# A hybrid attention decoder layer: three of sixteen gate projections computed beside the other attention

## Chip, cores and metric

The kernel runs on one core of a Trainium2 chip. The metric is the device time of one execution in microseconds. TensorE is called PE here (its weight loads PEld), VectorE DVE, ScalarE ACT, GpSimd POOL and SyncE SP, as in the profile.

## What is computed

One decoder layer on 1024 tokens of 1024 channels, all in float32. One input projection gives the queries, keys and values of two attention branches and two gates; branch A is a causal attention with a forget bias, branch B a sparse attention that keeps 256 keys per query; both are gated, summed, projected, and a SwiGLU follows.

```python
proj = x @ w_in[l]
(fq, fk, fv, f_logit, dq, dk, dv, iq, ik, iw, g_a, g_b) = _split_columns(proj)
o_a = _fox_attention(fq, fk, fv, f_logit + b_forget[l])     # 8 heads of 64
o_b = _dsa_attention(dq, dk, dv, iq, ik, iw)                # 8 heads of 64, top-k of indexer scores
...
merged = (jax.nn.sigmoid(g_a) * (o_a @ w_branch_a[l])
          + jax.nn.sigmoid(g_b) * (o_b @ w_branch_b[l]))
x = _layer_norm(ALPHA * x + merged @ w_out[l], ln1_g[l], ln1_b[l])
```

## The kernel before

Every float32 matmul is made of three: each operand is split into a high and a low part, and high x high, low x high and high x low are summed in PSUM (`mm3`, L99 to L101). A weight chunk of 128 columns is loaded by SP (L88), its high part made by ACT and its low part by POOL (`load_w`, L92 and L93).

After the input projections of the indexer come the two attentions, up to 800 us. They are done as 64 items in the order of the list `todo`: unit n (0 to 7) is a pair of heads, units 0 to 3 of the forgetting branch (items 0 to 31) and units 4 to 7 of the sparse branch (items 32 to 63); within a unit each of two heads goes through four pairs G of query blocks in the order 3, 0, 2, 1, so that four items in a row always make the same work, and the large ones are G = 3 and G = 2. An item has two parts. `weigh` makes the scores of its two query blocks (S, L456 to L459) and the softmax: for the forgetting branch a maximum on DVE (L466), an exponential on ACT (L467); for the sparse branch DVE adds the selection mask and takes the maximum (L469) and ACT makes the exponential (L472); then a reciprocal on DVE (L473) and the division on POOL (p, L476). `average` transposes p on PE (T, L499), splits the result on ACT (ph, L500) and DVE (pl, L501) and multiplies it with V (O, L508 and L509). The scores of the next item are made in the middle of the averaging of the present one, in slots; how many are before the transposes of the next item is fixed by `A1`.

Beside that PE does filler work: the projection of the next unit's queries, keys and values (48 steps) and the gate projections (16 steps each; 16 gates). A step is one `mm3` over 128 input channels for 512 tokens, three matmuls. A gate ends with two tanh evictions on ACT (L377) and two stores (L378). A projection of queries, keys and values ends with evictions on ACT and DVE (L392 and L393, L403 and L404, L428 and L429). `NG` says how many gates are done beside each unit; the steps of a unit are spread evenly over its eight items:

```python
total = [16 * g + (48 if n < 7 else 0) for n, g in enumerate(NG)]
...
    goal = sum(total[:n]) + total[n] * part // (2 * sum(W)) + lead * (64 - k) // 64
    for x, g in enumerate(slots):
        next(g, None)
        fill(work, at0 + (goal - at0) * (x + 1) // len(slots))
```

Beside each unit the gates come first, then the projection of the next unit.

PE's order is this order, word for word (`manual_schedule`). The other engines are ordered by a scheduler at build time that fills an engine whenever it finds it free. What it fills with in the forgetting half is the top-k selection, which needs only the indexer's scores: for query blocks 2, 3 and 4 by 32 rounds of max and replace on DVE (L287, L288), for blocks 5, 6 and 7 by a bisection of 32 rounds, in which ACT counts (L307) and DVE makes the next threshold (L308, L317, L315); at its end DVE turns the scores into a mask (L319 to L358). The sparse half begins only after that.

Of the kernel before, what the change touches and what calls it, by code (L numbers as in the profile page):

```python
# [36 lines left out]

NMM, NT = 2, 2
AHEAD, LASTC = 4, 6
NG = (1, 1, 2, 2, 2, 2, 2, 4)  # L40
ORDER = (3, 0, 2, 1)
PHB, PLB = 3, 3
A1 = (1, 2, 2, 2)
# [6 lines left out]
def trunk_kernel(ctx: ExitStack, tc: tile.TileContext, xT, xn, wt, wbr, wout, wfi, wfo,  # L50
# [506 lines left out]
    def filler():  # L557

        count = 0
        for n in range(8):  # L560
            for g in [gates.pop(0) for _ in range(NG[n])] + \
                    ([project(*divmod(n + 1, 4), units[n + 1])] if n < 7 else []):
# [8 lines left out]

    total = [16 * g + (48 if n < 7 else 0) for n, g in enumerate(NG)]
    done = [0]
# [395 lines left out]
```

## Time and profile before

| | us |
|---|---|
| median of 3 runs (1711.6 to 1712.47) | 1711.94 |
| the profiled execution | 1713.46 |
| its span, first to last instruction | 1711.70 |
| PE busy | 1632.9 |
| DVE busy | 1067.9 |
| ACT busy | 770.1 |
| POOL busy | 639.2 |

Busy time is the time in which an engine runs an instruction. Matmuls overlap in PE's pipeline, so how long one takes is read from the start of one to the start of the next. An engine works through its instructions in order; the time that it stood idle ahead of one is shown in brackets with what ended the wait.

### The profile page before, as it was taken

Reading aid. Unit: us, or ns where it says so; the run is one execution under the profiler, and the core shown is the slowest. Engines: PE = TensorE matmul, PEld = TensorE weight load, DVE = VectorE, ACT = ScalarE, POOL = GpSimd, SP = SyncE. Lnnn points to the kernel's source line nnn. Section 1 sums busy time; section 2 is a strip of 40 time slices with the busy share of each in tenths; the row PEclk is TensorE's granted clock in tenths of the full one; section 3 lists DMA queues with packets and bytes.
Section 4 is the critical chain, followed back from the end, with each engine's and each line's share of the span. In section 5 each row is a group of like instructions: output and inputs, shape, how many; then the busy total and the mean of one; then the engine's idle time right before and its main releaser. Section 6 shows DMA issues by size and latency. Waiting matters only on the chain.

```text
span 1711.7 us, 22054 instructions
## 1 busy us (share of the span) xinstructions
PE 1632.9 (95%) x7806; PEld 1335.1 (78%) x7806; DVE 1067.9 (62%) x1875; ACT 770.1 (45%) x1375; POOL 639.2 (37%) x617
## 2 busy tenths in 40 slices
PE   7898999998999999999989988999999998899998
PEld 5776887776888888887867866888888887788886
DVE  6889999969545454545376588744444443545655
ACT  6777878783545454455231033233333331433430
POOL 1123333332333333333340048644444442553751
PEclk9999999999999999999999998999999999899999
DMA  5112212221212121215875113322222220753641
GB/s 180 40 44 61 58 50 53 69 57 48 75 50 75 58 70 57 68 57 192 282 235 195 50 50 101 110 85 87 81 80 79 82 74 36 265 192 122 228 141 62
DMA packets 66326, 171.06 MB, mean 100 GB/s; under 512 B 7908, under 2 KB 12004, under 8 KB 66216
## 3 DMA queue, kind: packets, MB, share of 16 engines
q1 hardware_dynamic: 66216, 169.66, 30.6%
q8 instruction: 61, 1.00, 0.2%
q14 instruction: 49, 0.40, 0.1%
HBM read 123.67 MB, written 37.04 MB: 94 GB/s over the span
## 4 chain that ended last, share of the span: by engine, by line
PE 72%; DVE 13%; ACT 5%; DMA 4%; issue 3%; POOL 1%; SPq 0%; DVEq 0%; ACTq 0%; POOLq 0%
PE pb L100 8%; PE pb L101 8%; PE pb L99 8%; PE mm L99 6%; PE mm L100 6%; PE mm L101 6%; PE acc L100 5%; PE acc L99 5%; PE acc L101 5%; PE T L499 3%; PE ob L100 2%; PE ob L101 2%; PE ob L99 2%; DVE sm L288 2%; PE O L509 2%
## 5 line engine op out<-in xcount | busy, mean ns | idle before, releaser
L99 PE MATMUL mm<-xh,whi 128*128 128x512 f32 (+1 forms) x720 | 296.6, 412 | 15.6 <-ACT whi L144 6.2
L101 PE MATMUL mm<-xl,whi 128*128 128x512 f32 (+1 forms) x720 | 281.7, 392 | 0.8 <-DVE xl L154 0.7
L100 PE MATMUL mm<-xh,wlo 128*128 128x512 f32 (+1 forms) x720 | 281.2, 391 | 0.5 <-DVE wlo L145 0.5
L476 POOL TENSOR_SCALAR p<-p,st 128x512 f32<-128x512 f32 (+1 forms) x192 | 113.3, 599 | 321.3 <-DVE st L473 265.9
L93 POOL TENSOR_TENSOR wlo<-wraw,whi 128x1024 fp32r<-128x1024 f32 x51 | 123.1, 2414 | 192.7 <-ACT whi L92 192.5
L101 PEld LDWEIGHTS mm<-xl,whi 128*128 128x128 f32 x720 | 136.1, 189 | 31.8 <-DVE xl L154 2.0
L99 PEld LDWEIGHTS mm<-xh,whi 128*128 128x128 f32 x720 | 137.1, 190 | 30.1 <-issue 6.4
L776 POOL TENSOR_TENSOR w<-ss,w 128x512 fp32r<-128x512 f32 x88 | 118.8, 1357 | 106.4 <-ACT w L775 81.6
L99 PE MATMUL acc<-foh,hh 128*128 128x512 f32 x352 | 138.3, 393 | 10.8 <-ACT hh L883 10.8
L100 PEld LDWEIGHTS mm<-xh,wlo 128*128 128x128 f32 x720 | 137.4, 191 | 12.9 <-DVE wlo L145 1.0
L93 POOL TENSOR_TENSOR fol<-wraw,foh 128x1024 fp32r<-128x1024 f32 x44 | 108.2, 2464 | 101.3 <-ACT foh L92 70.3
L884 DVE TENSOR_TENSOR hl<-hr,hh 128x512 fp32r<-128x512 f32 x44 | 93.0, 2126 | 84.8 <-ACT hh L883 84.8
L100 PE MATMUL acc<-foh,hl 128*128 128x512 f32 x352 | 138.1, 392 | 0.0
L101 PE MATMUL acc<-fol,hh 128*128 128x512 f32 x352 | 137.9, 392 | 0.0
L501 DVE TENSOR_TENSOR pl<-T,ph 128x512 fp32r<-128x512 f32 (+1 forms) x160 | 100.6, 634 | 36.5 <-ACT ph L500 34.6
L776 POOL TENSOR_TENSOR w<-wraw,w 128x512 fp32r<-128x512 f32 x44 | 59.0, 1346 | 157.6 <-PE ob L101 86.2
L500 ACT ACTIVATE ph<-T 128x512 fp32r<-128x512 f32 (+1 forms) x160 | 87.2, 552 | 38.9 <-PE T L499 34.6
L307 ACT ACTIVATE junk<-sm,nt 128x1024 bf16<-128x1024 f32 (+2 forms) x93 | 96.8, 1041 | 14.6 <-DVE nt L315 12.8
L775 ACT ACTIVATE w<-ss 128x512 fp32r<-128x512 f32 x88 | 54.8, 629 | 102.4 <-PE pb L101 92.1
L499 PE MATMUL T<-identf,p 128*128 128x128 f32 x576 | 90.6, 273 | 4.8 <-POOL p L476 2.5
L499 PEld LDWEIGHTS T<-identf,p 128*128 128x128 f32 x576 | 71.2, 140 | 26.8 <-POOL p L476 4.5
L92 ACT ACTIVATE foh<-wraw 128x1024 fp32r<-128x1024 f32 x44 | 46.4, 1059 | 99.1 <-DMA wraw<-in_wfo_dram 56.9
(256 smaller groups left out, 3997.8 us busy)
## 6 DMA issues: line engine op xcount, KB each, us to landing
wraw<-in_wt_dram SPq DMA_DIRECT2D x45, 512.0 KB
wraw<-in_wfo_dram SPq DMA_DIRECT2D x44, 512.0 KB
wraw<-in_wfi_dram SPq DMA_DIRECT2D x26, 512.0 KB
wup<-in_wfi_dram SPq DMA_DIRECT2D x22, 512.0 KB
hdr<-h SPq DMA_DIRECT2D x22, 512.0 KB
hr<-hdr SPq DMA_DIRECT2D x44, 256.0 KB
gdr<-g SPq DMA_DIRECT2D x32, 256.0 KB
g<-gdr SPq DMA_DIRECT2D x32, 256.0 KB
```

The lines of the kernel that those rows point to most:

```text
L93: pool.tensor_tensor(lo, raw, f(hi), op=OP.subtract)
L99: te.matmul(ps, ah, bh, start=(first and i == 0), stop=False)
L100: te.matmul(ps, al, bh, start=False, stop=False)
L101: te.matmul(ps, ah, bl, start=False, stop=(last and i == n - 1))
L307: act.activation(j[:, :128 * (i + 1)], SM[i], AF.Sign, bias=bias(x), accum_out=s[:, x:x + 1])
L476: pool.tensor_scalar(pc, pc, st[:, 3:4], 1.0, op0=OP.mult, op1=OP.mult)
L499: te.transpose(T[:, s * 128:s * 128 + 128], P[qq][:, j * 128:j * 128 + 128], identf)
L500: act.activation(ph[:, c:], T[:, c:], AF.Copy)
L501: dve.tensor_tensor(pl[:, c:], T[:, c:], f(ph[:, c:]), op=OP.subtract)
L775: act.activation(s[:, 0], raw, AF.Copy)
L776: pool.tensor_tensor(s[:, 1], raw, f(s[:, 0]), op=OP.subtract)
L884: dve.tensor_tensor(hl, hr, f(hh), op=OP.subtract)
```

## The change

`NG`, the number of gates beside each unit, is changed. Beside the forgetting branch (units 0 to 3) there are nine gates instead of six, beside the sparse branch seven instead of ten.

```diff
-NG = (1, 1, 2, 2, 2, 2, 2, 4)
+NG = (1, 2, 3, 3, 1, 1, 2, 3)
```

What each group of items has beside it, counted in the built order (steps between the first score matmul of the first item and that of the item after the last; the other counts are DVE's instructions):

| items | before | after |
|---|---|---|
| 8 to 15 | 62 steps; 52 max and replace, 24 of the bisection, 12 projection evictions | 76 steps; 64, 28, 11 |
| 16 to 19 | 38 steps | 46 steps |
| 20 to 23 | 39 steps | 47 steps |
| 24 to 27 | 39 steps; the 59 instructions of the selection's end, 30 of attention, 4 projection evictions | 47 steps |
| 22 to 25 (second cycle's middle) | | 48 steps; the 59 instructions of the selection's end, 30 of attention, 9 projection evictions |
| 28 to 31 | 40 steps | 48 steps |
| 36 to 39 | 40 steps | 32 steps |
| 60 to 62 | 27 steps | 20 steps |

PE, forgetting half: the first place in which the two orders differ, in unit 1, after the last score of a block (S) and ahead of the transposes of p.

```order
 L458 MATMUL S<-cmask,identb 128x128
 L459 MATMUL S<-K_1378,Q_1377 128x256
+L99 MATMUL mm<-xh_79,whi 128x512
+L100 MATMUL mm<-xh_79,wlo 128x512
+L101 MATMUL mm<-xl_81,whi 128x512
 L499 MATMUL T<-identf,p 128x128 x4
```

One step more stands between the scores and the transposes.

PE, sparse half: what stands behind the second score of item 58 (unit 7), up to the first multiplication with V, before:

```order
L459 MATMUL S<-K_7158,Q_7157 128x384
L99 MATMUL mm<-xh_79,whi 128x512
L100 MATMUL mm<-xh_79,wlo 128x512
L101 MATMUL mm<-xl_81,whi 128x512
L99 MATMUL mm<-xh_79,whi 128x512
L100 MATMUL mm<-xh_79,wlo 128x512
L101 MATMUL mm<-xl_81,whi 128x512
L508 MATMUL O<-ph,V 128x256
```

and after:

```order
L459 MATMUL S<-K_7220,Q_7219 128x384
L99 MATMUL mm<-xh_79,whi 128x512
L100 MATMUL mm<-xh_79,wlo 128x512
L101 MATMUL mm<-xl_81,whi 128x512
L508 MATMUL O<-ph,V 128x256
```

Two steps have become one; the rest up to the transposes of item 58 is the same.

DVE, forgetting half: the first scan of the selection's end (L353, L354) with what stands among it, before:

```order
L353 SCALAR_TENSOR_TENSOR cum<-e 128x512
L501 TENSOR_TENSOR pl<-T,ph 128x512
L466 TENSOR_REDUCE st<-S 128x1
L354 SCALAR_TENSOR_TENSOR e<-cum,s_4393,e 128x512
L501 TENSOR_TENSOR pl<-T,ph 128x512
```

and after:

```order
L501 TENSOR_TENSOR pl<-T,ph 128x512
L404 TENSOR_TENSOR K_3271<-mm,K_3269 64x512
L354 SCALAR_TENSOR_TENSOR e<-cum,s_4573,e 128x512
L346 TENSOR_SCALAR s_4573<-s_4573 128x1
L501 TENSOR_TENSOR pl<-T,ph 128x512
L404 TENSOR_TENSOR K_3275<-mm,K_3273 64x512
L466 TENSOR_REDUCE st<-S 128x1
```

The evictions of a projection of keys (K, L404) now stand among the selection's end.

## Rows read from the trace of the kernel before

**Rows 1.** The page's slices: busy tenths of 40 equal slices of the span.

```profile
PE   7898999998999999999989988999999998899998
DVE  6889999969545454545376588744444443545655
```

**Rows 2.** Stretches: length, busy PE, PEld, DVE, ACT, POOL (count), clock, DMA share, GB/s.

```profile
216.00:292.80 76.80, 73.91 (x411) 59.56 (x410) 75.39 (x176) 62.17 (x129) 26.37 (x46) 1.00 0.20 57
292.80:336.00 43.20, 41.68 (x228) 33.74 (x227) 41.94 (x95) 35.81 (x72) 14.78 (x21) 1.00 0.16 56
336.00:378.70 42.70, 41.56 (x226) 33.96 (x225) 30.97 (x73) 36.87 (x76) 13.41 (x24) 1.00 0.27 69
378.70:431.40 52.70, 45.38 (x235) 35.67 (x234) 48.84 (x104) 23.25 (x49) 16.19 (x22) 0.97 0.14 46
431.40:473.20 41.80, 41.80 (x229) 34.57 (x228) 22.56 (x40) 20.40 (x41) 14.46 (x25) 1.00 0.27 71
```

**Rows 3.** PE's timeline: start us, us, instruction; two steps in a row.

```profile
419.52 0.40 PE L99 MATMUL mm<-xh,whi 128*128 128x512 f32 x1
...
420.21 0.39 PE L99 MATMUL mm<-xh,whi 128*128 128x512 f32 x1
```

**Rows 4.** PE's timeline: two of its waits, idle time and releaser in brackets.

```profile
385.87 0.47 PE L99 MATMUL mm<-xh,whi 128*128 128x512 f32 x1 [2.02 <-DVE V L429]
...
414.47 0.44 PE L456 MATMUL S<-K,Q 128*128 128x384 f32 x1 [2.05 <-ACT p L467]
```

**Rows 5.** DVE's timeline: first and last instruction of the selection's end.

```profile
386.15 0.16 DVE L319 TENSOR_SCALAR u<-u 128x3 int32<-128x3 int32 x1
...
430.42 2.64 DVE L358 TENSOR_SCALAR sm<-sm 128x256 f32<-128x256 f32 x1
```

**Rows 6.** Groups by line, 216 to 433 us: count, busy us, mean ns, idle before.

```profile
L287 DVE MAX8 m<-sm 128x8 f32<-128x640 f32 (+1 forms) x47 | 36.5, 776 | 0.2
...
L404 DVE TENSOR_TENSOR K<-mm,K 64x512 fp32r<-64x512 f32 x8 | 5.5, 686 | 2.4 <-ACT K L403 2.2
L429 DVE TENSOR_TENSOR V<-mm,V 128x256 fp32r<-128x256 f32 x10 | 4.1, 413 | 0.4 <-ACT V L428 0.3
...
L92 ACT ACTIVATE whi<-wraw 128x1024 fp32r<-128x1024 f32 x12 | 12.7, 1057 | 0.0
```

**Rows 7.** Timelines of DVE and POOL around 316 us.

```profile
316.46 1.81 DVE L315 SCALAR_TENSOR_TENSOR nt<-u,mp 128x3 int32<-128x3 int32 x1
...
315.86 2.39 POOL L93 TENSOR_TENSOR wlo<-wraw,whi 128x1024 fp32r<-128x1024 f32 x1 [3.65 <-ACT whi L92]
```

**Rows 8.** Timeline: first step after an item's second score, division, transposes (items 36, 58, 60).

```profile
520.53 0.40 PE L99 MATMUL mm<-xh,whi 128*128 128x512 f32 x1
...
524.83 1.36 POOL L476 TENSOR_SCALAR p<-p,st 128x512 f32<-128x512 f32 x2 [4.92 <-DVE st L473]
...
526.02 0.60 PE L499 MATMUL T<-identf,p 128*128 128x128 f32 x4
...
745.16 0.40 PE L99 MATMUL mm<-xh,whi 128*128 128x512 f32 x1
...
748.03 1.14 POOL L476 TENSOR_SCALAR p<-p,st 128x512 f32<-128x512 f32 x2 [3.00 <-DVE st L473]
...
748.75 0.60 PE L499 MATMUL T<-identf,p 128*128 128x128 f32 x4
...
762.02 0.40 PE L99 MATMUL mm<-xh,whi 128*128 128x512 f32 x1
...
765.37 1.36 POOL L476 TENSOR_SCALAR p<-p,st 128x512 f32<-128x512 f32 x2 [3.27 <-DVE st L473]
...
766.12 0.60 PE L499 MATMUL T<-identf,p 128*128 128x128 f32 x4
```

**Rows 9.** PE's timeline: a wait in the last item, at the multiplication with V.

```profile
798.41 0.38 PE L509 MATMUL O<-pl,V 128*128 128x256 f32 x1 [0.45 <-DVE pl L501]
```

## Prediction

> **What bounds the kernel now.** I read the page first. TensorE (PE) is the engine with the fewest gaps: a slice is 42.8 us, and its digits fall below 9 in slices 1, 2, 4 and 10 and then not before slice 18. VectorE's (DVE) digits are 8 and 9, with one 6, in slices 2 to 10 and only 3 to 5 in slices 11 to 20 [rows 1]. The two places that the change touches are the forgetting half (items 0 to 31, to 473 us) and the sparse half (items 32 to 63, to 800 us). To see what each costs I cut the trace at the first score matmul of every fourth item, because four items always make the same attention work, and read the busy times of each stretch [rows 2].
>
> In items 28 to 31 PE is busy for all of 41.8 us: nothing is waited for. That gives the price of four items with 40 steps of projection beside them, 41.8 us. One step (three matmuls) lasts 0.69 to 0.70 us from start to start [rows 3]. So PE's own time for four items with n steps is 41.8 - 0.70 x (40 - n), and what a stretch takes beyond that is waiting. With the steps counted in the order: items 8 to 15 have 62 steps, own time 71.0, taken 76.8, so 5.8 us of waiting; items 16 to 19 have 38, 40.4 of 43.2, 2.8; items 20 to 23 have 39, 41.1 of 42.7, 1.6; items 24 to 27 have 39, 41.1 of 52.7, 11.6 us. Together 21.8 us of waiting before the change [rows 2].
>
> Who is waited for: in items 8 to 15 DVE is busy for 75.39 of 76.8 us, and in items 24 to 27 for 48.84 of 52.7. DVE carries the top-k selection there beside the softmax, and PE waits for DVE's results (2.02 us for the eviction of V) or for a softmax that stood behind DVE (2.05 us) [rows 4]. The last part of the selection, L319 to L358, stands from 386.15 to 433.06 us [rows 5]; it is 40 us before the sparse half begins, so its end itself holds up nothing. In items 20 to 23 DVE has 12 us to spare; there ScalarE's counting passes set the pace (36.87 of 42.7 us busy), with little waiting.
>
> **What is moved.** 48 steps of 0.70 us, 33.5 us of PE time, leave the sparse half and go to the forgetting half. PE has to do them in either place, so this by itself is worth nothing: PE's total stays. The gates bring no DVE work, but each brings a weight load, its two splits (ScalarE and GpSimd, POOL), two tanh evictions and two stores. ScalarE has at least 5.8 us to spare in each stretch, POOL is busy for a third of each and DMA for at most 27% [rows 2], so I cost these at nothing. If that cover were gone, three splits at 1.06 us and six tanh evictions at no more than that would be 9.5 us of ScalarE [rows 6]. On SP's queue a store waits for its tanh, and the weight loads behind it wait with it; these are asked for while the chunk before is still being multiplied, 16 steps or 11 us ahead. What counts is how the waiting changes.
>
> Items 8 to 15. The order puts 76 steps there in place of 62: own time 80.8 us. But it also puts more selection there: 64 instead of 52 max and replace instructions and 28 instead of 24 of the bisection, less one eviction. A max takes 0.78 us [rows 6], and I take the replace that follows each alike; one of the bisection's small ones takes 0.16 [rows 5]; an eviction 0.69. This is 12 x 0.78 + 4 x 0.16 - 0.7 = 9.3 us, and DVE comes to 75.4 + 9.3 = 84.7, still more than PE's own time. With the 1.4 us that the stretch took beyond DVE's busy time, 86.1 us, and 5.3 us of waiting instead of 5.8. Bounds: 1.6 (as in items 20 to 23, if DVE just stops binding) and 6.4.
>
> Items 16 to 21. The counting passes set the pace, as before in items 20 to 23 with 1.6 us per four items: 2.4 us for six items. Before, eight items had 4.4. Bounds 1.0 and 4.4.
>
> The selection's end. Its 59 instructions stand beside the scores of items 22 to 25 now, instead of items 24 to 27. PE has 48 steps there, own time 47.4 us. DVE has the same 59, the same 30 of attention, and nine instead of four evictions of projections, since the projection of the next pair of heads falls into the same place: four more of K at 0.69 us and one of V at 0.41, 3.2 us [rows 6]. If the stretch takes 52.7 + 3.2 = 55.9 us, the wait is 8.5 us, 3.1 less than before. But the load is uneven: counted up to the first score of item 25, DVE's instructions add up to 9 us more than PE's; with the 3.9 us by which this stretch exceeded DVE's busy time before, that is 13. I take 10.5, between them; ends 8.5 and 14.8 (nothing of the longer PE work helps, 11.6 + 3.2).
>
> Items 26 to 31 wait for nothing, as items 28 to 31 do now. Sum for the forgetting half: 5.3 + 2.4 + 10.5 = 18.2 us of waiting instead of 21.8: 3.6 us gained (between 10.7 gained and 3.8 lost).
>
> One thing speaks against the move. At 316.46 a DVE instruction on three numbers per partition took 1.81 us; a weight split on POOL had begun 0.60 us before it, and both ended at about 318.25 [rows 7]. About one more split (one per 16 steps) now falls before the selection's end: 0 to 1.7 us of DVE time, and I take 0, since the busy times above hold such hits already. The Trainium skill (SBUF — State Buffer, Who interferes with whom) says that a DVE instruction with two SBUF inputs and a GpSimd instruction that reads SBUF exclude each other for the whole instruction; the trace agrees. By that rule alone every added split could cost its full length once, and the forecast would be about 2 us later.
>
> The sparse half. There PE never waits, but by little. Between an item's second score and its transposes the chain runs over DVE, ScalarE, DVE and POOL, and PE must have that much other work. At item 58 PE's work lasts 748.75 - 745.16 = 3.59 us and the chain to the end of POOL's first of two instructions 748.60 - 745.16 = 3.44; at item 60, 4.10 and 4.03; at item 36, 5.49 against 4.98 [rows 8]. The change takes one step out of this gap at items 58 and 60 and two at items 62, 36, 40 and 44. So items 58 and 60 wait 0.6 us each, and item 62, which is like item 58 with one step more in the gap and loses two, 0.6 as well. Items 36, 40 and 44 come to 4.1 us against chains of 4.0 to 5.0: 0 to 0.9 each, I take 0.2, since most chains are at the low end. The last pair waits 0.45 us already [rows 9]; with a step less, 0.6 more. Together 3.0 us lost, bounds 1.5 and 7.
>
> **The sum.** 3.6 gained and 3.0 lost: 0.6 us faster. The profiled execution took 1713.46 us, 1.76 of it around the span of 1711.70, and would come to 1712.9. It lies 1.5 us above the median of 1711.94, and against the median I say 1711.3 us.
>
> **The rivals.** Faster: the denser filler gives DVE so much more time per item that it no longer binds in items 8 to 21, and the selection's end takes the lower end. Then 1.6 + 1.5 + 8.5 = 11.6 us of waiting are left, 10.2 gained, less 3.0: 1711.9 - 7.2 = 1704.7 us. For it: from item 8 to the end of the selection PE's own work is 193.6 us beside 197.1 of DVE busy [rows 2]; with the change the selection ends two items earlier but with 15 steps more done, 10.5 us of PE less the attention of two items, while DVE's load shrinks by the softmax of two items. Summed over the whole, PE would be the longer. Against it: the order lets the selection run ahead whenever PE is slower, so DVE stays full where it was full.
>
> Slower: the thin gap in the sparse half. If chains like item 36's (4.98) are the rule once items follow each other faster, because evictions and tanh come between, the twelve large items of units 4, 5 and 7 wait 0.5 us more each, and 9 us are lost instead of 3.0: 1711.9 - 3.6 + 9.0 = 1717.3 us. It decides from the point where the chain is longer than PE's work in the gap, 4.1 us in units 4 and 5 and 2.9 to 3.4 in unit 7. For it: item 36, 0.5 us from waiting with two steps more. Against it: items 58 and 60 ran at the shorter chains at eight steps per item.
>
> Nothing: the waits move along with the selection, their sum stays near 21.8, and the sparse half loses nothing that can be measured: 1711.9 us. This lies in the same band as the forecast.
>
> **Chances.** A measurement of this kernel tells about 0.2%, 3.4 us, from no change. Forecast 0.34, nothing 0.11, together 0.45 for the same; faster 0.31; slower 0.24. The bounds of the terms add up to -9.2 and +10.8 us, which is not likely on one side at once; 1704.5 to 1718.0 holds the rivals' times and leaves out about two in ten.
>
> **What would show it.** In the trace of the changed kernel: the sparse half, from the first score of item 32 to that of item 60, shorter by the moved work; items 8 to 15 at about 86 us with DVE full; the stretch with L319 to L358 as the one with most waiting, some 10 us; PE waits of about 0.6 us for POOL's p at the transposes of items 58, 60 and 62. I am wrong if the stretch with the selection's end shows under 6 us of waiting or over 14, or if the large items of units 4 and 5 wait too.

## The result, and the profile after

The changed kernel takes 1721.59 us (median of 4 runs, 1720.76 to 1722.84) against 1712.20 for the kernel before beside it: ratio 1.0053, 95% interval 1.0036 to 1.0071. It is slower by 9 us, and outside the range of the prediction. The profiled execution took 1722.84 us, 1721.1 of it span, 9.4 more than the span before.

The page's slices for PE and DVE hardly differ from [rows 1]:

```profile
PE   7899999998999999999998988999999999899998
DVE  6889999969345454555375689744444443455655
```

So the trace was cut again at the first score matmuls, with the columns of [rows 2]. These are items 8 to 15, 16 to 19, 20 to 23, 24 to 27 and 28 to 31 of the changed kernel:

```profile
216.00:301.10 85.10, 82.48 (x453) 67.41 (x452) 83.39 (x194) 67.26 (x138) 28.85 (x47) 1.00 0.21 63
301.10:349.10 48.00, 47.30 (x253) 38.37 (x252) 43.75 (x100) 38.97 (x80) 15.60 (x22) 1.00 0.20 66
349.10:402.40 53.30, 48.30 (x251) 38.20 (x250) 39.86 (x92) 35.75 (x72) 16.09 (x23) 1.00 0.22 61
402.40:455.60 53.20, 48.68 (x259) 39.05 (x258) 32.99 (x62) 20.24 (x43) 17.18 (x23) 1.00 0.16 55
455.60:503.00 47.40, 47.40 (x254) 39.09 (x253) 20.66 (x38) 21.91 (x44) 15.45 (x23) 1.00 0.26 74
```

Items 28 to 31 again wait for nothing. The selection's end stands where it was forecast, in items 22 to 25; the first and last instruction on DVE's timeline, to be held against [rows 5]:

```profile
378.37 0.17 DVE L319 TENSOR_SCALAR u<-u 128x3 int32<-128x3 int32 x1
...
426.51 0.28 DVE L358 TENSOR_SCALAR sm<-sm 128x256 f32<-128x256 f32 x1
```

The new thing is in the sparse half. PE's waits there (us in total, times, longest), 503 to 808 us:

```profile
PE T L499 <- POOL p L476: 6.1, 7, 1.3
PE ob L99 <- ACT g L377: 2.3, 1, 2.3
```

Before, the same list, from 473 to 801.5 us so that it too takes in the branch stage's first matmul (`ob`):

```profile
PE ob L99 <- ACT g L377: 0.7, 1, 0.7
PE O L509 <- DVE pl L501: 0.5, 1, 0.5
```

**A ledger.** Moved steps lengthen one stretch and shorten another by 0.70 us each. What a stretch's length changed beyond that is a loss (+) or a gain (-). Here it is against the kernel before, for the changed kernel and all that was run, from one profiled execution each. The stretches begin at the first score of item 0, of item 32 and of item 56, at the branch stage's first matmul, and at the first matmul behind that stage and the output projection, which is counted with it. For the changed kernel the first entry, for example, is 29.7 us longer for 46 steps more: 29.7 - 32.2 = -2.5.

| kernel | items 0-31 | items 32-55 | item 56 to branch stage | branch stage | rest | ratio of times |
|---|---|---|---|---|---|---|
| changed kernel | -2.5 | +5.7 | +3.5 | +2.0 | +0.6 | 1.0053 |
| e1_low_on_dve | -2.7 | +3.7 | +3.6 | -0.6 | -0.2 | 1.0025 |
| e2_early6 | -2.6 | +0.7 | +3.4 | +1.8 | +1.0 | 1.0013 |
| e3_late2 | -2.6 | +0.5 | +3.6 | +1.4 | 0.0 | 1.0008 |
| e4_unit4_only | -6.6 | +2.0 | +0.2 | -0.7 | +0.2 | 0.9969 |
| e5_unit4_late2 | -5.9 | +0.1 | +0.6 | -1.4 | +0.6 | 0.9958 |
| e6_unit7_only | -6.5 | 0.0 | +3.6 | +0.9 | +0.6 | 0.9983 |
| e7_unit2 | -4.7 | +1.7 | +0.2 | +1.3 | +0.3 | 0.9980 |
| e8_unit3 | +1.1 | +1.7 | +0.8 | -0.3 | +1.0 | 1.0006 |
| e9_two_u12 | -2.4 | +0.5 | +0.3 | +0.8 | +0.7 | 0.9994 |
| e10_two_u1 | -5.0 | +0.5 | -0.2 | +1.1 | +0.5 | 0.9975 |
| e11_two_u01 | -7.0 | +0.6 | 0.0 | -0.7 | +0.4 | 0.9961 |
| e12_cast_dve | -2.5 | +5.7 | +1.9 | +3.6 | +0.7 | 1.0039 |

The row of the changed kernel adds up to 9.3 of the 9.4 us. The runs' ratios have intervals of about 0.001 to each side; a ledger's sum, which rests on one execution of each kernel, lies up to 3.3 us from what its ratio says. Beside the experiments the kernel before took 1714.6 to 1715.1 us, some 2.5 us more than beside the changed kernel, which did not run again; so times are compared as ratios.

### The profile page after: what moved, and what is told of

Read it like the earlier page. It is cut to its first block, busy times and chain, and to the rows that moved or that the text cites. A ratio compares the mean times of both kernels' runs of the same rounds, so it can differ in the third digit from the quotient of the medians.

```text
span 1721.1 us, 22044 instructions
## 1 busy us (share of the span) xinstructions
PE 1633.4 (95%) x7806; PEld 1334.7 (78%) x7806; DVE 1068.8 (62%) x1875; ACT 769.9 (45%) x1375; POOL 641.4 (37%) x617
## 4 chain that ended last, share of the span: by engine, by line
PE 71%; DVE 15%; ACT 6%; issue 3%; DMA 3%; POOL 2%; SPq 0%; DVEq 0%; ACTq 0%; POOLq 0%
PE pb L100 8%; PE pb L101 8%; PE pb L99 8%; PE mm L99 6%; PE mm L101 6%; PE mm L100 6%; PE acc L99 5%; PE acc L100 5%; PE acc L101 5%; PE T L499 3%; PE ob L100 2%; PE ob L101 2%; PE ob L99 2%; DVE sm L288 2%; DVE m L287 2%
## 5 line engine op out<-in xcount | busy, mean ns | idle before, releaser
L476 POOL TENSOR_SCALAR p<-p,st 128x512 f32<-128x512 f32 (+1 forms) x192 | 113.8, 601 | 326.1 <-DVE st L473 287.5
L499 PE MATMUL T<-identf,p 128*128 128x128 f32 x576 | 91.7, 274 | 10.4 <-POOL p L476 8.0
L499 PEld LDWEIGHTS T<-identf,p 128*128 128x128 f32 x576 | 71.0, 140 | 33.2 <-POOL p L476 11.3
```

What stands on the lines that cost most here:

```text
L476: pool.tensor_scalar(pc, pc, st[:, 3:4], 1.0, op0=OP.mult, op1=OP.mult)
L499: te.transpose(T[:, s * 128:s * 128 + 128], P[qq][:, j * 128:j * 128 + 128], identf)
```

## The experiments

**What stood in the chain.** Item 40 of the changed kernel, on the timeline of all engines: its last score matmul (L459), the softmax over DVE, ACT, DVE (L469, L472, L473), the division on POOL (L476) and PE's transposes (L499).

```profile
583.04 0.40 PE L459 MATMUL S<-K,Q 66*128 66x512 f32 x1
...
584.67 1.05 ACT L92 ACTIVATE whi<-wraw 128x1024 fp32r<-128x1024 f32 x1
...
585.62 1.14 ACT L472 ACTIVATE p<-p,st 128x1024 f32<-128x1024 f32 x1
585.81 2.39 POOL L93 TENSOR_TENSOR wlo<-wraw,whi 128x1024 fp32r<-128x1024 f32 x1 [2.23 <-ACT whi L92]
...
586.88 0.17 DVE L473 RECIPROCAL st<-st 128x1 f32<-128x1 f32 x1 [1.73 <-ACT p L472]
...
587.39 0.27 PE L499 MATMUL T<-identf,p 128*128 128x128 f32 x1
...
588.18 1.71 POOL L476 TENSOR_SCALAR p<-p,st 128x512 f32<-128x512 f32 x3
...
588.93 0.55 PE L499 MATMUL T<-identf,p 128*128 128x128 f32 x3 [1.26 <-POOL p L476]
```

And item 40 of the kernel before:

```profile
561.12 0.40 PE L459 MATMUL S<-K,Q 66*128 66x512 f32 x1
...
563.44 1.14 ACT L472 ACTIVATE p<-p,st 128x1024 f32<-128x1024 f32 x1
...
564.57 1.05 ACT L92 ACTIVATE whi<-wraw 128x1024 fp32r<-128x1024 f32 x1
564.70 0.16 DVE L473 RECIPROCAL st<-st 128x1 f32<-128x1 f32 x1 [1.62 <-ACT p L472]
564.96 1.36 POOL L476 TENSOR_SCALAR p<-p,st 128x512 f32<-128x512 f32 x2 [3.95 <-DVE st L473]
...
566.28 2.39 POOL L93 TENSOR_TENSOR wlo<-wraw,whi 128x1024 fp32r<-128x1024 f32 x1
```

The same instructions, in another order. Before, ACT's cast of the next weight chunk and POOL's low part stand behind the softmax's instructions. After, the cast stands ahead of the exponential, and the low part ahead of the division, which then starts 1.30 us after its reciprocal is there (588.18 against 586.88) instead of 0.26. From the end of the last score matmul to the start of the division it is 4.74 us after, 3.44 before, while PE's work in that gap, from 583.44 to the first transpose at 587.39, has become 3.95 us. A chunk lasts 16 steps. With 8 steps per item it lasts two items exactly, so that the split stands between the two blocks' divisions of every even (large) item from 32 to 44; at 10 steps the place drifts, and before it stood there at items 32, 34 and 42 of these. The place alone does not make a wait, the moment counts too: before, at item 42, the split ran from 582.46 to 584.87 us, and the reciprocal came only at 585.18; in the changed kernel items 32 and 34 met the split without a wait, as PE had 5.7 us of work at the one, and the division was only 0.6 us late at the other.

Nor is it the split in every item that waits. Item 36 of the changed kernel, beginning at its last score matmul:

```profile
546.49 0.40 PE L459 MATMUL S<-K,Q 66*128 66x512 f32 x1
546.61 0.69 DVE L393 SCALAR_TENSOR_TENSOR Q<-mm,Q 64x512 fp32r<-64x512 f32 x1 [0.38 <-ACT Q L392]
...
547.61 2.41 POOL L93 TENSOR_TENSOR wlo<-wraw,whi 128x1024 fp32r<-128x1024 f32 x1 [0.79 <-ACT whi L92]
548.59 0.69 DVE L393 SCALAR_TENSOR_TENSOR Q<-mm,Q 64x512 fp32r<-64x512 f32 x1
...
550.84 0.16 DVE L473 RECIPROCAL st<-st 128x1 f32<-128x1 f32 x1 [0.74 <-ACT p L472]
551.11 1.71 POOL L476 TENSOR_SCALAR p<-p,st 128x512 f32<-128x512 f32 x3 [1.09 <-DVE st L473]
```

Here the split is over before the softmax is, and the division follows its reciprocal by 0.27 us. The reciprocal itself is late, 3.95 us behind the last score (546.89), where item 36 of e3 below has 2.93: two evictions of the projection on DVE (L393) stand in the chain. They come after every 8 steps of a projection, so they too keep their place at 8 steps per item. Item 38 has the same with K (L404). So of the five items that wait, two wait for evictions and three, items 40, 42 and 44, for cast and split (with one eviction at item 44).

Theory T1: the split's place in the chain costs the 5.7 us of items 32 to 55. R1: 8 steps are too few for the chain wherever the split stands. R2: the loss comes at the end. e1 takes POOL's part of the split out of POOL's queue:

```diff
+    low = [pool]
     def load_w(src, hi=None, lo=None):
...
-        pool.tensor_tensor(lo, raw, f(hi), op=OP.subtract)
+        low[0].tensor_tensor(lo, raw, f(hi), op=OP.subtract)
...
         for n in range(8):
+            low[0] = dve if n >= 4 else pool
...
+        low[0] = pool
```

> The changed kernel, with one thing other: the low parts of the weight chunks loaded in units 4 to 7 are made on DVE instead of POOL. Nothing else moves. The changed kernel takes 1721.6 us, the kernel before 1712.2. Theory T1 (in units 4 and 5 each weight split stands in the chain from scores to transposes: POOL's 2.39 us row ahead of the division, which then starts 1.3 to 1.5 us after its reciprocal): the chain of items 36, 40, 42, 44 falls from 5.1-5.6 us to about 4.3, their waits at the transposes from 5.0 us in sum to about 1, and the time to about 1717.5. Rival R1 (8 steps and a gap of 4.1 us are too few for the chain wherever the split stands): waits stay near 5 us, time 1721.6. Rival R2 (the loss comes at the end, in the step into the branch stage and behind it): waits and time unchanged, 1721.6.

Measured: 1.0025 (1.0014 to 1.0036). PE's waits for the division from 503 to 655 us fell from 4.3 to 1.9 us. Item 40 again:

```profile
583.24 0.40 PE L461 MATMUL S<-K,Q 66*128 66x512 f32 x1
...
585.82 1.14 ACT L474 ACTIVATE p<-p,st 128x1024 f32<-128x1024 f32 x1
585.96 1.23 DVE L95 TENSOR_TENSOR wlo<-wraw,whi 128x1024 fp32r<-128x1024 f32 x1 [0.61 <-ACT whi L94]
...
587.10 0.15 DVE L475 RECIPROCAL st<-st 128x1 f32<-128x1 f32 x1
587.35 1.36 POOL L478 TENSOR_SCALAR p<-p,st 128x512 f32<-128x512 f32 x2 [3.58 <-DVE st L475]
```

The division starts 0.25 us after the reciprocal, 3.71 us after the last score. In items 40, 42 and 44 the waits fell from 3.6 to 0.7 us. But the cast is still ahead of the exponential, items 36 and 38 still wait (0.9 and 0.4 us) for the evictions, and 3.7 of the 5.7 us are still lost: T1 was right on the place, and I had put too much of the price on POOL alone. The rest of the time that e1 won lies in the branch stage, where no theory had it.

e2 and e3 leave every instruction where it is made and move the chunk's boundary against the items. The line, with SHIFT 6 (e2) or -2 (e3):

```diff
-        goal = sum(total[:n]) + total[n] * part // (2 * sum(W)) + lead * (64 - k) // 64
+        goal = sum(total[:n]) + total[n] * part // (2 * sum(W)) + lead * (64 - k) // 64 + (SHIFT if n in (4, 5) else 0)
```

> The changed kernel, with one thing other: in units 4 and 5 the projection steps run 6 steps ahead of where they stood (the goal of each item there is 6 higher), so a chunk of 16 steps ends 6 steps earlier against the items; the steps per item stay at 8. By the order of POOL's instructions the split then stands ahead of the first block's division of the large items 34 to 48 instead of between their two blocks. T1: the waits at items 36 to 44 fall from 5.2 us to 1 or less, and the time by about 4 to 1717.5. R1: waits as before the shift, 1721.6. R2: 1721.6.

> The changed kernel, with one thing other: in units 4 and 5 the projection steps run 2 steps behind where they stood, so that POOL makes the split after the large item's two divisions and ahead of the first block of the small item that follows (35, 37, ... 49). The chain of a small item is shorter on DVE and POOL, but its split stands in it now. T1: the waits of the even items 36 to 44 vanish (5.2 to under 1 us), those of the odd items appear with at most 0.5 us each; time 1717 to 1719.5. R1: 1721.6 with the same even items waiting. R2: 1721.6.

Measured: e2 1.0013 (1.0004 to 1.0021), e3 1.0008 (1.0000 to 1.0017). In both, the list of PE's waits from 503 to 655 us is empty of waits for the division, and the ledger shows 0.7 and 0.5 instead of 5.7. In e3 the split stands behind item 40's division, which starts 3.40 us behind the last score, and the four transposes follow each other:

```profile
580.42 0.40 PE L459 MATMUL S<-K,Q 66*128 66x512 f32 x1
...
583.97 0.17 DVE L473 RECIPROCAL st<-st 128x1 f32<-128x1 f32 x1 [1.37 <-ACT p L472]
584.23 1.36 POOL L476 TENSOR_SCALAR p<-p,st 128x512 f32<-128x512 f32 x2 [3.24 <-DVE st L473]
...
584.76 0.76 PE L499 MATMUL T<-identf,p 128*128 128x128 f32 x4
...
584.86 1.05 ACT L92 ACTIVATE whi<-wraw 128x1024 fp32r<-128x1024 f32 x1
...
585.99 2.40 POOL L93 TENSOR_TENSOR wlo<-wraw,whi 128x1024 fp32r<-128x1024 f32 x1 [0.41 <-ACT whi L92]
```

R1 and R2 fall for this stretch: with the same 8 steps per item the waits are gone as soon as the chunk's boundary stands elsewhere. The odd items did not wait in its place. The shift moves the cast and the evictions together with the split, so e2 and e3 show that the place decides, not which of the three; the split's own share is what e1 took away. Both ratios are 3 us or more below T1's times, while the ledger's gain of about 5 us is as T1 has it; what the rest is stays open.

**One part alone.** e4, e6, e7 and e8 move one gate, from the kernel before:

```diff
-NG = (1, 1, 2, 2, 2, 2, 2, 4)
+NG = (1, 2, 2, 2, 1, 2, 2, 4)
```

This is e4; in e6 the table is (1, 2, 2, 2, 2, 2, 2, 3), in e7 (1, 1, 3, 2, 1, 2, 2, 4), in e8 (1, 1, 2, 3, 1, 2, 2, 4).

> One gate alone moves against the kernel before: from unit 4 to unit 1, so that unit 4 has 8 steps per item and units 5 and 7 stay at 10 and 8. The kernel before takes 1712.2. T1: items 36, 38 and 40 wait about 0.9, 0.2 and 1.4 us, against 0.6 in sum before; unit 5 at 10 steps does not wait; the forgetting half gives 1 back (a third of 2.4); 1713 (1712.0 to 1714.0). R1: the same waits in unit 4 whatever the split's place, 1713 as well; the time alone does not tell them apart here, the place of the split in the trace does. R2 (loss at the end): unit 4 costs nothing, 1711.2.

Measured: 0.9969 (0.9957 to 0.9982), faster than the kernel before, where each theory had 1711 to 1713 us. Items 32 to 55 lost 2.0, near the 1.9 of T1, with waits at items 36, 38 and 40 alone (0.9, 0.5 and 0.3 us). The miss is in the forgetting half: I had given this gate a third of the 2.4 us that three gates earned, and alone it earned 6.6.

e5 is e4 with SHIFT -2 in unit 4 alone.

> Against the kernel before: one gate moves from unit 4 to unit 1 (as in e4_unit4_only), and in unit 4 the steps run 2 behind, so that POOL makes the splits of items 34 to 41 behind the large item's divisions. e4 measured 0.9969 of the kernel before (5.3 us faster), with 1.8 us more waiting than before in units 4 and 5. T1 (split in the chain): these 1.8 us go too, 0.9958 to 0.9964 of before (6 to 7 us faster). R1 (gap too thin): as e4, 0.9969.

Measured: 0.9958 (0.9946 to 0.9971), median 1707.46 against 1714.85 of the kernel before beside it, the fastest kernel of all. The 2.0 us of unit 4 are gone (+0.1), with no wait for the division left from 478 to 634 us. The intervals of e4 and e5 overlap; it is the traces that tell T1 from R1 here.

> Against the kernel before: one gate alone moves from unit 7 to unit 1. The forgetting half should gain what it gained in e4 (6.4 us: 11.2 of steps, 4.8 later at item 32). Theory T4 (the thinner last unit is what costs at the end: 0.8 in items 56 to 59, 2.5 in item 60 to the branch stage, 1 to 2 in the branch stage, as in the changed kernel): net 1.5 us faster, ratio 0.9990 (0.9980 to 1.0000). Rival (the end's 2.5 and 2.0 come from the offset of the transfers and not from the unit being thinner): only 0.8 is lost, net 5.6 us faster, 0.9967.

Measured: 0.9983 (0.9974 to 0.9992). The ledger shows +3.6 from item 56 to the branch stage as in the changed kernel, and -0.2 to +0.8 in the seven kernels that leave unit 7 its four gates: it is the thinner last unit that costs this, as T4 says.

> Against the kernel before: one gate moves from unit 4 to unit 2 (e4 moved the same gate to unit 1). Theory T3 (a gate in unit 2 puts its evictions and splits beside the selection's end, and PE then waits 5 to 6 us in items 22 to 24, as in the changed kernel): the forgetting half gains 0 to 1.5 instead of 6.4, unit 4 loses 1.8; ratio 0.9995 to 1.0010. Rival (only how much work lies ahead of the selection's end counts, not the unit): as e4, 0.9969.

> Against the kernel before: one gate moves from unit 4 to unit 3, whose items 24 to 31 lie across the selection's end. By the trace of the changed kernel against e4 (items 24 to 31 take 100.6 us there with 3 gates, 91.2 in e4 with 2: 9.4 more for 11.2 of steps) a gate in unit 3 gains 1.8. T3: gain 1.8 less unit 4's loss of 1.8: ratio 1.0000 (0.9990 to 1.0010). Rival (the selection's end takes any work moved ahead of item 32): as e4, 0.9969.

Measured: e7 0.9980 (0.9971 to 0.9989), e8 1.0006 (0.9997 to 1.0014). T3 foresaw the time of e8, but with a term that was off: the gate in unit 3, which it had earn 1.8, lost 1.1 us. For e7 it was wrong: the gate in unit 2 earned 4.7 us; items 22 and 23 did not wait, and item 24 waited 4.0.

**Do the gains add?** 6.6, 4.7 and -1.1 us would be 10.2 for three gates, and the changed kernel has 2.5. e9, e10 and e11 move two gates and have SHIFT -2 in units 4 and 5:

```diff
-NG = (1, 1, 2, 2, 2, 2, 2, 4)
+NG = (1, 2, 3, 2, 1, 1, 2, 4)
```

This is e9; in e10 the table is (1, 3, 2, 2, 1, 1, 2, 4), in e11 (2, 2, 2, 2, 1, 1, 2, 4).

> Against the kernel before: two gates move, one from unit 4 to unit 1 and one from unit 5 to unit 2; units 4 and 5 run 2 steps behind, so that the splits stand behind the large items' divisions; unit 7 keeps its 4 gates. Alone, the gate in unit 1 gave 6.4 us back in the forgetting half, the one in unit 2 gave 4.8, one in unit 3 gave nothing; all three together, in the changed kernel, 2.4. Theory T5 (the gains add, and it was the gate in unit 3 that took them back): 11 us faster, ratio 0.9936. Rival (they do not add: DVE is busy from 387 to 426 us whatever moves, and with two gates ahead PE waits some 12 us again in items 22 to 26, as in the changed kernel): 1 to 3 us faster, 0.9982 to 0.9994.

> Against the kernel before: two gates move, both to unit 1, from units 4 and 5; units 4 and 5 run 2 steps behind as in e9. T5 (work put into unit 1 keeps PE fed until the selection's end): 9 to 12 us faster, ratio 0.9930 to 0.9948. Rival (the second gate earns nothing; items 8 to 15 have 4.6 us of waits left and DVE sets the stretch to 426 us): as e5, 0.9958, or back to 0.9985 if 12 us of waits return at the selection's end.

> Against the kernel before: two gates move, one to unit 0 (items 0 to 7 hold 6.6 us of waits) and one to unit 1, from units 4 and 5; units 4 and 5 run 2 steps behind as in e9. T5: 9 to 12 us faster, 0.9930 to 0.9948. Rival (not additive): as e5, 0.9958, or back to 0.9985 if 12 us of waits return at the selection's end.

Measured: 0.9994 (0.9985 to 1.0003), 0.9975 (0.9965 to 0.9985) and 0.9961 (0.9948 to 0.9975). The gains don't add; T5 fell. In e9 the waiting in items 22 to 25 is 12.4 us, as in the changed kernel, which the rival had foreseen. The stretch from 387 to 426 us of e4, the changed kernel and e9, one row of each (columns as in [rows 2]):

```profile
387.00:426.00 39.00, 35.09 (x183) 28.18 (x182) 38.39 (x80) 13.47 (x29) 13.58 (x15) 0.96 0.15 46
```

```profile
387.00:426.00 39.00, 30.84 (x158) 23.38 (x159) 38.55 (x71) 14.06 (x31) 12.73 (x15) 1.00 0.19 54
```

```profile
387.00:426.00 39.00, 32.29 (x160) 24.64 (x161) 38.58 (x71) 14.03 (x30) 12.39 (x14) 0.96 0.19 54
```

DVE is full in all three. What PE gets done beside it differs: 183, 158 and 160 matmuls. A gate ahead of the stretch gains what PE doesn't wait in it; which rows fall there is set by all units together. What decides it in the single case stays open, but one thing goes along with it. DVE's instructions take longer beside a POOL split ([rows 7] has one). Counted over items 0 to 31 against the median of each form in all the traces, this is 12.3 us before, 11.6 in the changed kernel and in e9, and 9.6, 6.8, 8.2 and 8.7 in e4, e7, e10 and e11, the four that earned 4.7 to 7.0 there. e8, with 9.8, does not fit, and no run here moves these splits alone, so this is not shown to be the cause.

**The end.** In the changed kernel the branch stage's first matmul waits 2.3 us for the last gate's tanh, which stands on ACT behind a cast of the stage's operand. e12 is the changed kernel with that cast, the third, on DVE:

```diff
-            act.activation(oh[k], raw, AF.Copy)
+            (dve.tensor_copy(oh[k], raw) if br == 0 and k == 2 else act.activation(oh[k], raw, AF.Copy))
```

> The changed kernel, with one thing other: the third cast of the branch stage's first operand is made on DVE, so that it no longer stands ahead of the last gate's tanh on ACT. Theory T4 (the 2.3 us wait at the first matmul of the branch stage comes from that cast, which waits 0.86 for its load and takes 1.06): the wait falls to about 0.7 and the time by 1.6, to 1720.0, ratio 1.0044. Rival (the wait comes from elsewhere, or DVE's cast delays the branch stage by as much): 1.0053, as the changed kernel.

Measured: 1.0039 (1.0026 to 1.0051). Its interval overlaps that of the changed kernel, and its span is 0.4 us shorter (1720.7). The first matmul waits 0.69 us instead of 2.30, and a later matmul of the same group waits 2.37 us for the same operand. DVE's timeline, and PE's:

```profile
806.10 0.69 DVE L534 CAST oa<-oraw 128x1024 fp32r<-128x1024 f32 x1 [0.82 <-DMA oraw<-odr]
```

```profile
805.81 0.50 PE L99 MATMUL ob<-oa,whi 128*128 128x512 f32 x1 [0.69 <-ACT g L377]
...
810.28 0.70 PE L101 MATMUL ob<-oa,whi 128*128 128x512 f32 x1 [2.37 <-DVE oa L535]
```

So T4 was right about the first wait: with the cast off ACT it is 0.69 us, as before the change. That this won so little time has another reason. The low part that the later matmul waits for took 3.40 us on DVE, against 1.23 in the changed kernel; a split of the next weight chunk had begun on POOL 0.04 us ahead of it:

```profile
806.79 2.37 POOL L93 TENSOR_TENSOR wlo<-wraw,whi 128x1024 fp32r<-128x1024 f32 x1 [8.84 <-ACT whi L92]
806.83 3.40 DVE L535 TENSOR_TENSOR oa<-oraw,oa 128x1024 fp32r<-128x1024 f32 x1
```

The new wait of 2.37 us came of this meeting; in the changed kernel the split began at 808.85, after the low part. The time does not tell T4 from its rival, whose second half (the stage delayed by as much) is what the trace shows. The third cast itself waited for its load, 0.86 us in the changed kernel and 0.82 in e12. The first two loads of this operand are issued about when the last score matmul ends (before at 787.95 us, 0.7 behind it; after at 794.92), and the third cast starts 11.2 to 11.4 us after that (799.35 and 806.14). From there to PE's last step there were 13.2 us of work before and 10.5 after. That the last unit's steps covered these loads is my reading; e6 shows only that the thinner unit costs this.

## Why the prediction was wrong, by its own steps

**Forgetting half: right in the main.** Forecast 18.2 us of waiting and 3.6 gained. By the same reckoning (the stretch less 41.8 - 0.70 x (40 - n) per four items) it is now 4.3 us in items 8 to 15 (85.1 us; 86.1 were forecast), 2.7 in items 16 to 21 (the pair G = 3 and 0 takes 1.0 us more than half of four items), 12.4 in items 22 to 25 and none behind: about 19.4, 2.4 gained. The selection's end took most, within its bounds of 8.5 to 14.8. The sum was near, but the reason was incomplete: a single gate earns 6.6 us in unit 1 and loses 1.1 in unit 3 (e4, e8), and a sum near 0 came from gains and losses that the steps did not hold apart. The 0 for the added splits was right: three more splits stand in this half, and what DVE lost beside splits was 12.3 us before and 11.6 after. So the sentence on the Trainium skill's page SBUF — State Buffer weighs a cost that could come and, in sum, did not.

**The chain in units 4 and 5: the step that failed.** Items 36, 40 and 44 were put at 4.1 us of PE's work against chains of 4.0 to 5.0, 0.2 us of waiting each, and items 38 and 42 at none; with this the chain of the kernel before was carried over, as if its neighbours on DVE, ACT and POOL stayed where they were. The gap that PE's work leaves was right: measured 3.94 to 4.14. The chain was not. Items 36, 38, 40, 42 and 44 waited 0.9, 0.2, 1.4, 1.2 and 1.4, 5.2 together (by the spacing of PE's starts beyond the usual one): at 8 steps per item the evictions, the cast and the split fell into the chain item after item. With the chunk's boundary elsewhere the forecast's low end was right (0.5 and 0.7 lost in e3 and e2). I had asked what the splits cost only in the forgetting half, and answered with busy shares: POOL is busy for a third of each stretch. That is an average. POOL and ACT work in order, and a split 2.39 us long in front of a division delayed it by 1.3 us at item 40 however idle POOL is over the stretch. The change did not add a split to the sparse half, it took three away; it changed where they stand. The order of POOL's instructions in both kernels showed the place beforehand (between the two blocks' divisions at all even items from 34 to 44 after, at 34 and 42 before), though not the moment.

**Sparse half: 3.0 forecast, 9.2 taken (5.7 and 3.5).** The 5.7 are the step above. In unit 7 items 58, 60 and 62 were to wait 0.6 each. PE's timeline, at their transposes (the pieces that answer to [rows 8]):

```profile
761.26 0.55 PE L499 MATMUL T<-identf,p 128*128 128x128 f32 x3 [0.52 <-POOL p L476]
...
776.50 0.55 PE L499 MATMUL T<-identf,p 128*128 128x128 f32 x3 [0.42 <-POOL p L476]
...
792.27 0.55 PE L499 MATMUL T<-identf,p 128*128 128x128 f32 x3 [0.83 <-POOL p L476]
```

By the spacing these are 0.7, 0.6 and 1.0 us, so that was near; at item 62 the split stood between the divisions again. (Item 58's chain was read as 3.44 us by halving POOL's 1.14; its first instruction takes 0.69, which makes 3.57.) The last pair, which was to wait 0.6 us more, did not wait at all. What was missed behind them is 1.6 us more of waiting at the branch stage's first matmul (2.30 instead of 0.69), behind the cast for the third load of its operand, which no step named: the prediction followed the last item to its own end only.

**The rest.** I had nothing behind the sparse half; 2.6 us were lost there. The branch stage's length varies from 1.4 us less to 3.6 more than before over these kernels and does not follow the gates moved (+1.8 in e2, -0.6 in e1, with the same gates). Taken together with the column ahead of it, though, the six kernels with three gates in unit 7 lose 3.0 to 5.5 us, and the seven with four between -0.8 and +1.5. What sets the stage's length is open.

**The rivals.** The slower one had the place right (the thin gap in units 4, 5 and 7) and came nearest to the time, 1717.3 against 1721.6; I had given it a chance of 0.24. Its cause, evictions that come between, is what items 36 and 38 show (1.1 us); the cast and the split of items 40 to 44 it did not have. "I am wrong if the large items of units 4 and 5 wait too" is what happened. The low end of the range was also shown reachable, by other numbers for the same table and a shift: e5, at 0.9958.

## What to carry to other kernels

An engine that is two thirds idle still costs its longest background instruction when that stands in a latency chain (1.3 us at item 40); so read the order, and the moment, on each in-order queue around the chain, not the busy share. A change of rate that makes a background period (16 steps) a whole multiple of the foreground's (two items) locks the two together, and what met one large item now and then meets every one in a row; shifting the phase cured it in e2, e3 and e5. And a term that looks like one sum, here three gates, is worth pricing gate by gate: one earned between -1.1 and 6.6 us, two between 2.4 and 7.0, three 2.5.

## What was not expected of the hardware

In e8 PE did little in 414 to 417 us (it waited 2.3 us), and was then busy but at the lower clock for some 6 us; stretches of 3 us, with the granted clock third from the end:

```profile
414.00:417.00 3.00, 1.02 (x5) 0.51 (x3) 2.96 (x5) 0.60 (x1) 0.00 (x0) 1.00 0.59 165
417.00:420.00 3.00, 2.67 (x8) 2.17 (x9) 2.93 (x7) 1.15 (x4) 1.76 (x2) 0.51 0.32 121
420.00:423.00 3.00, 3.00 (x9) 2.32 (x8) 2.90 (x6) 0.78 (x1) 0.00 (x0) 0.50 0.01 3
423.00:426.00 3.00, 3.00 (x15) 2.50 (x13) 2.96 (x7) 0.60 (x3) 2.07 (x2) 0.85 0.00 0
```

At 0.50 of full speed, the lower of the two levels, a step took 1.28 us from start to start there, against 0.70; by the clock column the last 9 us hold 5.6 us at full speed, so some 3.4 were lost behind the wait, an estimate. It is not what sets e8 apart: e7 shows as much (clock 0.66 over 395 to 403 us, 0.92 over the next 8), and its gate earned 4.7 us; the kernel before shows half (0.79 over 411 to 419). In the changed kernel, with waits of up to 1.8 us in the same stretch, the clock stayed at 1.00.

The same 128x1024 low part took 1.23 us on DVE (e1) and 2.39 on POOL, and a like subtract on DVE 3.40 beside a split on POOL (e12).
